# Down projections of two feed-forward layers: three groups of four chunks by seven products of quarters, between plain pairs

## The chip, the core and the metric

The program runs on one core of a Trainium2 chip. The time is the device time of one execution in microseconds, the median of several runs. A profiled execution gives the rows that are quoted. Engines: PE (TensorE matrix multiplication, with its weight loads as PEld), DVE (VectorE), ACT (ScalarE), POOL (GpSimd), and SP, whose queue issues nearly all transfers.

## What is computed

Three transformer blocks follow one another on 1024 tokens of width 1024 in 32-bit floats. Blocks 1 and 3 end in a feed-forward layer of 2816 inner channels:

```python
# first block: causal convolution over three tokens on the up projection
up = causal_depthwise_conv(h @ w_up[l], conv_w[l], conv_b[l])
a, bgate = jnp.split(up, [D_FF], axis=-1)
x = x + (jax.nn.silu(a) * bgate) @ w_down[l]
# third block
gate, up = jnp.split(h @ w_gate_up, 2, axis=-1)
ffn = (jax.nn.silu(gate) * up) @ w_down
h = layer_norm_3(ALPHA * h + ffn, ln2_g[l], ln2_b[l])
```

The change concerns the products with `w_down` (2816 x 1024) in both layers. The function `ffn` writes both.

## The kernel before

Activations lie transposed, channels on the 128 partitions and tokens along the row, in two halves of 512 tokens. A 32-bit product is made from three passes: every operand is split into a high part, which ACT rounds (`ghi`, `whi`, `shi`), and a low part, the operand less its high part (`glo`, `wlo`, `slo`), made on POOL or DVE; PE adds high x high, low x high and high x low in one PSUM bank. One matmul is 128 x 128 by 128 x 512.

**The up projection** goes by seven products (Strassen's scheme in Winograd's form) in `strassen`: each weight tile of 1024 columns is cut in quarters, `s_steps` adds and subtracts them on POOL in six steps and splits them, and seven products take the place of eight. Its gated results `g` go out to DRAM (`gd<-g`).

**The down projection** comes behind it. The 2816 inner channels are 22 chunks of 128. The first 18 are taken as nine pairs in `down`: for each of eight row tiles `j` and two halves, six matmuls add two chunks into a fresh PSUM bank (`dn`; six banks in rotation, tag `b`), and DVE adds the bank to the running sum `X` (64 kept tiles of 128 x 512, tag `h`, hold `X`, `gx` and their parts). The four last chunks go another way, which stays as it is. For each pair two weight tiles are loaded (`raw`), split on ACT and POOL, and two chunks by two halves of gated products are read back (`gx<-gd`), and split, two on POOL and two on DVE. The work left from the last step of `strassen` (`self.left`: four convolutions with their gates in the first layer, one gate in the third) is done at every third group of the first pair.

**Order.** Instructions stand in the order in which Python writes them, engine by engine; nothing is reordered. SP's queue holds each transfer until its buffer is free, and what stands behind it waits too. `tail` issues, during the last seven-product step of the up projection, the loads of the first weights, of the first gated products and of `X`.

Of the kernel before, what the change touches and what calls it, by code (L numbers as in the profile page):

```python
# [9 lines left out]
F32 = mybir.dt.float32  # L10
F32R = mybir.dt.float32r
AF = mybir.ActivationFunctionType
ALU = mybir.AluOpType
# [7 lines left out]
NFF = FF // 128  # L21
# [18 lines left out]
def _weights(a):  # L40
    def wa(name, lo, hi):
        return list(_chunks_a(a[name][0][:, lo:hi]))

    def wb(name, lo, hi):
        return list(_chunks_b(a[name][0][:, lo:hi]))

    def abba(tiles):
        return tiles + tiles[0:4]

    def ffn(up, down):  # L50
        ab = _chunks_a(a[up][0])
# [247 lines left out]
class Kernel:  # L299
# [14 lines left out]
    def bank(self, name="bank"):  # L314
        return self.ps.tile([128, 512], F32, tag="b", name=name)
# [957 lines left out]

    def s_dma(self, n):

        pool = self.up if (n + self.lead) % 2 else self.wp
# [82 lines left out]
    def ffn(self, evac, put, later, add_last, done, by_half, alpha=None, lead=2):  # L1359
# [3 lines left out]
        nc, X, G = self.nc, self.X, {}  # L1363
        from contextlib import ExitStack
        with ExitStack() as ctx:
# [33 lines left out]
            def g_group(i):  # L1399
                cs = (2 * i, 2 * i + 1) if i < NFF // 2 - 2 else range(NFF - 4, NFF)  # L1400
                return [(c, half, i % 2 and c < NFF - 1) for c in cs for half in range(2)]

            def x_load(j):
                for half in range(2):
                    X[j][half] = self.h("X")
                    nc.sync.dma_start(out=X[j][half], in_=self.x2d[j][:, HF * half:HF * half + HF])

            def tail(n):

                if n == 0:  # L1410
                    del self.stops[0]
                    self.wi += 2 * (NFF - lead)
                    self.w_load()
                    self.w_load()
                elif n == 1:
                    for a in g_group(0):
                        g_dma(*a[:2])
                    for j in range(2):
                        x_load(j)
                elif n == 2:  # L1420
                    for j in range(2, 5):
                        x_load(j)
                else:
                    for a in g_group(0):
                        g_split(*a, nc.gpsimd)
# [24 lines left out]
            def down(i, ws):  # L1450
                n = 0
                loads = g_group(i + 1)
                gap = 12 // len(loads)
                for j in range(8):
                    for half in range(2):
                        ps = self.bank("dn")
                        for k in range(2):
                            whi, wlo = ws[k]
                            ghi, glo = G[2 * i + k, half]
# [6 lines left out]
                        if alpha and i == 0:  # L1466
# [9 lines left out]
            for i in range(NFF // 2 - 2):  # L1476
                ws = self.w_take(2)
                if i == 0:
                    self.w_retire(0)
                yield from down(i, ws)  # L1480
                if i < NFF // 2 - 3:
                    for a in g_group(i + 2):
                        g_dma(*a[:2])
                self.w_retire(2)
# [1018 lines left out]
```

## Time and profile before

| | us |
|---|---|
| median of 3 runs | 3134.41 (3132.58 to 3134.44) |
| profiled execution, device time | 3128.57 |
| its span | 3126.8 |
| PE busy in the span | 2948.0 |
| POOL busy in the span | 1428.8 |

The down projection of the first layer begins at 904 us of the span, that of the third at 2850 us. A row of the timeline has start, duration, engine, line and operation, out<-in with sizes, and in brackets the engine's idle time before it and what ended it.

### The profile page before, as it was taken

The page shows a single profiled execution, that of the slowest core. Times are in us where ns is not written, and L with a number is a line of the kernel's source. Part 1 is how long each engine was busy: PE and PEld are TensorE (multiplying, and loading weights), DVE is VectorE, ACT ScalarE, POOL GpSimd, SP SyncE. Part 2 cuts the span into 40 slices and gives each one's busy share as a digit, 9 for nine tenths or more (in the row PEclk, how much of TensorE's full clock was granted, in tenths as well). Part 3 has the DMA queues.
Part 4 walks back from the last instruction along what each step waited for, and adds up shares of the span by engine and source line. Part 5 has one row for each costly group of instructions (what it writes and reads, how often), then busy time and mean ns, then how long its engine had stood idle before and what let it go on. Part 6 is the DMA issues. An engine that isn't in the chain of part 4 may idle for free. (4 is left out here: it accounts for less than half of the span.)

```text
span 3126.8 us, 41448 instructions
## 1 busy us (share of the span) xinstructions
PE 2948.0 (94%) x15222; PEld 2506.4 (80%) x15222; DVE 1797.5 (57%) x3512; ACT 1284.2 (41%) x2493; POOL 1428.8 (46%) x1006
## 2 busy tenths in 40 slices
PE   8999998999999999889998989998899899999997
PEld 7898776888878878868897778977688688888887
DVE  6444246666675569976645665577767522224556
ACT  4232224444431143556673356654444422222223
POOL 4313434777743365862214342144333477774330
PEclk9999999999999999999999999999889999999998
DMA  4101241222252312131113232110223222225321
GB/s 160 29 27 50 73 135 41 81 81 81 81 184 86 108 48 81 38 108 49 47 39 118 84 121 64 42 31 28 68 68 98 84 81 81 86 80 179 108 81 55
DMA packets 114876, 248.96 MB, mean 80 GB/s; under 512 B 19696, under 2 KB 31600, under 8 KB 114672
## 3 DMA queue, kind: packets, MB, share of 16 engines
q1 hardware_dynamic: 114384, 246.01, 24.0%
q8 instruction: 120, 1.97, 0.3%
q14 instruction: 84, 0.69, 0.1%
q10 hardware_dynamic: 288, 0.30, 0.0%
HBM read 192.52 MB, written 53.74 MB: 79 GB/s over the span
## 5 line engine op out<-in xcount | busy, mean ns | idle before, releaser
L332 POOL TENSOR_TENSOR wlo<-raw,whi 128x1024 fp32r<-128x1024 f32 x240 | 581.8, 2433 | 861.7 <-ACT whi L326 845.0
L326 ACT ACTIVATE whi<-raw 128x1024 fp32r<-128x1024 f32 x240 | 248.2, 1053 | 535.9 <-PE dn L347 283.7
L332 DVE TENSOR_TENSOR X<-dn,X 128x512 f32<-128x512 f32 (+1 forms) x312 | 209.8, 676 | 162.2 <-PE dn L347 159.9
L347 PE MATMUL dn<-ghi,whi 128*128 128x512 f32 (+1 forms) x736 | 281.7, 383 | 0.5 <-DVE X L332 0.5
L347 PE MATMUL dn<-glo,whi 128*128 128x512 f32 (+1 forms) x736 | 279.8, 380 | 0.0
L347 PE MATMUL dn<-ghi,wlo 128*128 128x512 f32 (+1 forms) x736 | 279.8, 380 | 0.0
L332 POOL TENSOR_TENSOR raw<-raw 128x512 f32<-128x512 f32 x156 | 203.0, 1301 | 12.1
L332 POOL TENSOR_TENSOR slo<-raw,shi 128x512 fp32r<-128x512 f32 x117 | 150.6, 1301 | 105.6 <-ACT shi L326 104.4
L347 PE MATMUL p<-thi,shi 128*128 128x512 f32 x468 | 184.7, 395 | 13.4 <-DVE u L1132 9.7
L332 DVE TENSOR_TENSOR v<-p,e 128x512 f32<-128x512 f32 x78 | 53.8, 689 | 243.6 <-ACT e L326 194.2
L347 PE MATMUL p<-hhi,wlo 128*128 128x512 f32 x468 | 182.2, 389 | 1.7 <-POOL wlo L332 1.7
L347 PE MATMUL p<-tlo,shi 128*128 128x512 f32 x468 | 183.2, 391 | 0.0
L347 PE MATMUL p<-thi,slo 128*128 128x512 f32 x468 | 183.1, 391 | 0.0
L347 PE MATMUL p<-hhi,whi 128*128 128x512 f32 x468 | 182.1, 389 | 0.0
L347 PE MATMUL p<-hlo,whi 128*128 128x512 f32 x468 | 182.1, 389 | 0.0
L329 DVE SCALAR_TENSOR_TENSOR t<-u,vec,t 128x512 f32<-128x512 f32 x176 | 132.9, 755 | 79.4 <-ACT t L326 74.1
L347 PE MATMUL qk<-hhi,whi 128*128 128x512 f32 x384 | 164.5, 429 | 7.7 <-ACT hhi L326 7.0
L332 POOL TENSOR_TENSOR beta<-beta,f 128x511 f32<-128x511 f32 (+3 forms) x96 | 90.3, 945 | 155.7 <-DVE beta L336 146.5
L347 PEld LDWEIGHTS dn<-ghi,whi 128*128 128x128 f32 x736 | 138.8, 189 | 27.9 <-DVE X L332 0.9
L347 PEld LDWEIGHTS dn<-glo,whi 128*128 128x128 f32 x736 | 138.7, 188 | 26.3
L347 PEld LDWEIGHTS dn<-ghi,wlo 128*128 128x128 f32 x736 | 138.6, 188 | 26.1
L347 PE MATMUL qk<-hlo,whi 128*128 128x512 f32 x384 | 154.9, 403 | 1.3 <-DVE hlo L329 1.3
(404 smaller groups left out, 8156.9 us busy)
## 6 DMA issues: line engine op xcount, KB each, us to landing
raw<-in_wall SPq DMA_DIRECT2D x240, 512.0 KB, 3.8
gd<-g SPq DMA_DIRECT2D x88, 256.0 KB, 2.1
gx<-gd SPq DMA_DIRECT2D x88, 256.0 KB, 5.1
x2d<-X SPq DMA_DIRECT2D x64, 256.0 KB, 2.0
X<-x2d SPq DMA_DIRECT2D x64, 256.0 KB, 5.3
x<-in_xT SPq DMA_DIRECT2D x16, 256.0 KB, 5.9
X<-in_xT SPq DMA_DIRECT2D x16, 256.0 KB, 4.1
T<-in_rpbx SPq DMA_DIRECT2D x8, 448.0 KB, 4.1
```

The lines of the kernel that those rows point to most:

```text
L326: self.nc.scalar.activation(out=out, in_=in_, func=func, bias=bias, scale=scale, **kw)
L329: self.nc.vector.scalar_tensor_tensor(out=out, in0=in0, scalar=s, in1=in1, op0=op0, op1=op1)
L332: (eng or self.nc.vector).tensor_tensor(out=out, in0=in0, in1=in1, op=op)
L347: self.nc.tensor.matmul(out=out, lhsT=lhsT, rhs=rhs, start=start, stop=stop, skip_group_check=more)
```

## The change

In place of nine pairs there are three rounds, each of one pair (function `two`, 16 groups of six matmuls as before) and one group of four chunks (two calls of `seven`, 14 groups of six matmuls each). The order of chunks is 2, 4, 2, 4, 2, 4, and the last four as before. I call the three parts of a round the pair, the first and the second half; each half serves half of the row tiles.

For a group of four, the weights are laid out on the host so that a tile holds 256 output channels of four chunks, and `s_steps` makes the sums of quarters on POOL, as in the up projection. The gated products' sums (`b_steps`: 5, 6, 7 and 4 are differences, 1, 2 and 3 plain) are made on DVE, one at a time between the evacuations; their high parts are ACT's, the low parts of the differences DVE's, those of the plain ones POOL's. In `seven`, bank `c` takes products 1, 6, 7 and 4 on top of one another; DVE adds what stands in it to `X` after each, and PE goes on in the same bank. Products 5 and 3 share `f`, product 2 has `d`, each with two banks, six in all. The work left from the up projection is done in the first groups of the first pair, one function at each. Loads change places: only two weight tiles are loaded ahead of the first gated products, then two tiles for the first half among `X`, and eight `gx` behind `X` in place of four.

```diff
@@ in _weights, ffn
-        out.extend(dn[:NFF - 4])
+        for i in range(0, NFF - 4, 6):
+            out.extend(dn[i:i + 2])
+            for col in (0, 512, 256, 768):
+                out.append(np.concatenate([dn[k][:, col:col + 256] for k in range(i + 2, i + 6)], axis=1))
-S_TILES = ((38, 38), (178, 180))
+S_TILES = ((38, 38), (78, 78), (178, 180), (220, 220))
@@ in Kernel.ffn
+            pairs = [(i, i + 1) for i in range(0, NFF - 4, 6)]
+            quads = [range(i + 2, i + 6) for i in range(0, NFF - 4, 6)]
...
                 elif n == 1:
-                    for a in g_group(0):
-                        g_dma(*a[:2])
+                    g_raw(pairs[0])
                     for j in range(2):
                         x_load(j)
+                    self.s_raws(self.up)
...
-                    for a in g_group(1):
-                        g_dma(*a[:2])
+                    g_raw(quads[0])
+                    self.s_raws(self.wp)
...
+                def raw(n, o, half):
+                    return [lambda k=k: self.tt(*pair(n, k, G[cs[o + k], half]), ALU.subtract, nc.gpsimd)
+                            for k in range(2)]
+
+                def made(n, out, parts):
+                    low = {}
+
+                    def diff(k):
+                        p, q = parts(k)
+                        x = out(k)
+                        self.tt(x, p, q, ALU.subtract)
+                        low[k] = pair(n, k, x)
+
+                    return [lambda: diff(0), lambda: diff(1), lambda: self.tt(*low[0], ALU.subtract),
+                            lambda: self.tt(*low[1], ALU.subtract)]
...
+                return (raw(1, 0, 0) + made(5, bank, lambda k: (G[cs[k], 1], G[cs[k], 0])),
+                        made(6, lambda k: t[k], lambda k: (G[cs[2 + k], 1], t[k])) + raw(2, 2, 0) +
+                        made(7, lambda k: G[cs[k], 1], lambda k: (G[cs[2 + k], 1], G[cs[k], 1])),
+                        raw(3, 2, 1) + made(4, lambda k: t[k], lambda k: (G[cs[2 + k], 0], t[k])))
...
@@ in two (was down)
-                        if n % 3 == 1 and self.left:
-                            self.left.pop(0)()
-                        if n % gap == 0 and loads and n > 2:
-                            g_split(*loads.pop(0))
+                        if self.left:
+                            self.left.pop(0)()
+                        for f in todo.get(n, ()):
+                            f()
...
+            def seven(s, A, B, todo):
+                banks, n = {}, 0
+                plan = ((1, "c", "A1", 0, 0, 0), (5, "f", "S1", 0, 4, 1), (6, "c", "S24", 0, 0, 1),
+                        (2, "d", "A1", 512, 0, 0), (7, "c", "S3", 0, 4, 1), (3, "f", "S24", 512, 0, 1),
+                        (4, "c", "A22", 0, 4, 0))
+                for p, key, w, off, row, half in plan:
+                    for m in range(2):
+                        start = (key, m) not in banks
+                        if start:
+                            banks[key, m] = self.bank("dn")
+                        ps = banks[key, m]
...
+                            self.mm(ps, whi[:, c], hi, start and k == 0, False, not start)
+                            self.mm(ps, whi[:, c], lo, False, False, not start)
+                            self.mm(ps, wlo[:, c], hi, False, k == 1, not start)
...
+                        self.tt(x, ps, x, ALU.add)
+                        for f in todo.get(n, ()):
+                            f()
+                        n += 1
...
+                        at((0, 2, 4, 6, 8, 10) if s is None else (0, 1, 2, 5, 7, 10), self.s_steps(u + 1, nxt))
+                if s is None:
+                    if u == 0:
+                        at((2, 3, 4, 5, 6, 7), b0)
+                    at((8, 9, 10, 11, 9, 11, 12, 13, 14, 15) if u == 0 else (0, 1, 3, 4, 5, 6, 7, 9, 11, 13), b1)
+                elif s == 0:
+                    at((0, 1, 1, 3, 5, 7), b2)
...
+                elif more:
+                    at((0, 1, 2, 3), [lambda c=c, h=h: g_split(c, h, False, nc.gpsimd)
+                                      for c in pairs[i + 1] for h in range(2)])
+                    nb = {}
+                    b0, b1, b2 = b_steps(quads[i + 1], nb)
+                    at((5, 6, 7, 9, 11, 13), b0)
```

The numbers in `at` are the groups of six matmuls after which a step is written.

The next rows show DVE at the start of the first layer's down projection. Of before, from the first evacuation on (`STT` work on `t` and `g` belongs to the convolutions):

```order
L332 TENSOR_TENSOR X<-dn,X 128x512
L1132 MEMSET u 128x2
L1134 COPY carry<-u 128x2
L329 SCALAR_TENSOR_TENSOR t<-u,vec,t 128x512 x2
L332 TENSOR_TENSOR X<-dn,X 128x512 x3
L1136 COPY u<-carry 128x2
L329 SCALAR_TENSOR_TENSOR t<-u,vec,t 128x512 x2
L332 TENSOR_TENSOR X<-dn,X 128x512 x2
L332 TENSOR_TENSOR glo<-gx,ghi 128x512
```

Of the change, from the second evacuation on:

```order
L335 TENSOR_TENSOR X<-dn,X 128x512
L1139 COPY u<-carry 128x2
L332 SCALAR_TENSOR_TENSOR t<-u,vec,t 128x512 x2
L335 TENSOR_TENSOR X<-dn,X 128x512
L1135 MEMSET u 128x2
L1137 COPY carry<-u 128x2
L332 SCALAR_TENSOR_TENSOR t<-u,vec,t 128x512 x2
L335 TENSOR_TENSOR g<-t,a 128x512
L335 TENSOR_TENSOR X<-dn,X 128x512
L1139 COPY u<-carry 128x2
L332 SCALAR_TENSOR_TENSOR t<-u,vec,t 128x512 x2
L335 TENSOR_TENSOR g<-t,a 128x512
```

The convolutions now stand behind each of the first four evacuations, where they stood behind the first, the fourth, the seventh and the tenth.

POOL, of before, from a pair's weights to the next pair's (`raw` are weight tiles, `gx` gated products):

```order
L332 TENSOR_TENSOR wlo_7499<-raw_7294,whi_7498 128x1024
L332 TENSOR_TENSOR wlo_7505<-raw_7300,whi_7504 128x1024
L332 TENSOR_TENSOR glo_7544<-gx_7454,ghi_7543 128x512
L332 TENSOR_TENSOR glo_7617<-gx_7458,ghi_7616 128x512
L332 TENSOR_TENSOR wlo_7697<-raw_7502,whi_7696 128x1024
L332 TENSOR_TENSOR wlo_7703<-raw_7508,whi_7702 128x1024
```

Of the change, in the second round's pair (the steps for the first half, and product 2's low parts among them):

```order
L335 TENSOR_TENSOR slo_8083<-raw_7920,shi_8082 128x512
L335 TENSOR_TENSOR raw_7920<-raw_7920 128x512
L335 TENSOR_TENSOR raw_7920<-raw_7918,raw_7920 128x512
L335 TENSOR_TENSOR slo_8130<-raw_7920,shi_8129 128x512
L335 TENSOR_TENSOR slo_8134<-raw_7920,shi_8133 128x512
L335 TENSOR_TENSOR glo_8147<-gx_7889,ghi_8146 128x512
L335 TENSOR_TENSOR wlo_8159<-raw_7918,whi_8158 128x1024
L335 TENSOR_TENSOR glo_8163<-gx_7893,ghi_8162 128x512
L335 TENSOR_TENSOR raw_7918<-raw_7920,raw_7918 128x512
L335 TENSOR_TENSOR raw_7918<-raw_7918 128x512
L335 TENSOR_TENSOR wlo_8209<-raw_7918,whi_8208 128x1024
```

Two low parts of 1024 columns and two of 512 were a pair's whole work; now a pair has eleven operations on POOL, four of them sums of quarters on `raw`.

DVE, of before, in the first layer's second pair:

```order
L332 TENSOR_TENSOR X_7334<-dn_7708,X_7334 128x512
L332 TENSOR_TENSOR X_7336<-dn_7716,X_7336 128x512
L332 TENSOR_TENSOR X_7338<-dn_7724,X_7338 128x512
L332 TENSOR_TENSOR X_7340<-dn_7736,X_7340 128x512
L332 TENSOR_TENSOR X_7390<-dn_7744,X_7390 128x512
L332 TENSOR_TENSOR X_7392<-dn_7752,X_7392 128x512
```

Of the change, in the first half of the first round (`dn_7748` and `dn_7764` are the two banks `c`):

```order
L335 TENSOR_TENSOR X_7330<-dn_7748,X_7330 128x512
L335 TENSOR_TENSOR X_7334<-dn_7764,X_7334 128x512
L335 TENSOR_TENSOR t_7606<-gx_7462,t_7606 128x512
L335 TENSOR_TENSOR X_7400<-dn_7782,X_7400 128x512
L335 TENSOR_TENSOR X_7444<-dn_7798,X_7444 128x512
L335 TENSOR_TENSOR t_7619<-gx_7466,t_7619 128x512
L335 TENSOR_TENSOR X_7332<-dn_7748,X_7332 128x512
L335 TENSOR_TENSOR X_7336<-dn_7764,X_7336 128x512
L335 TENSOR_TENSOR glo_7780<-t_7606,ghi_7779 128x512
L335 TENSOR_TENSOR X_7330<-dn_7837,X_7330 128x512
L335 TENSOR_TENSOR X_7334<-dn_7845,X_7334 128x512
```

Each evacuation read a bank of its own; now bank `dn_7748` is read, written on and read again, and the differences (`t`) and their low parts stand between.

## Rows read from the trace of the kernel before

**Rows 1.** Page, section 1: busy us, share of the span, instructions.

```profile
PE 2948.0 (94%) x15222; PEld 2506.4 (80%) x15222; DVE 1797.5 (57%) x3512; ACT 1284.2 (41%) x2493; POOL 1428.8 (46%) x1006
```

**Rows 2.** Busy time by stretch: up projection, then down projection of the first layer.

```profile
core 0: us, PE busy (x) PEld busy (x) DVE busy (x) ACT busy (x) POOL busy (x), PEclk, DMA share, GB/s
...
700.00:750.00 50.00, 50.00 (x222) 41.42 (x221) 33.37 (x57) 23.79 (x36) 37.49 (x26) 1.00 0.20 69
...
904.00:925.00 21.00, 20.48 (x90) 16.59 (x89) 16.29 (x29) 7.21 (x11) 8.60 (x6) 1.00 0.70 265
925.00:946.00 21.00, 21.00 (x93) 17.14 (x92) 15.03 (x24) 4.55 (x6) 7.82 (x4) 1.00 0.50 163
...
967.00:988.00 21.00, 21.00 (x94) 17.39 (x93) 11.57 (x18) 4.09 (x6) 7.27 (x4) 1.00 0.30 101
```

**Rows 3.** Waits of PE, 2840 to 3110 us, then 880 to 1160 us.

```profile
PE ln L347 <- DVE lsq L332: 2.6, 1, 2.6
...
PE dn L347 <- DVE X L332: 0.5, 1, 0.5
```

**Rows 4.** Timeline of PE, first and second pair of the first layer.

```profile
904.00 0.39 PE L347 MATMUL dn<-ghi,whi 128*128 128x512 f32 x1
...
922.38 0.50 PE L347 MATMUL dn<-ghi,whi 128*128 128x512 f32 x1 [0.52 <-DVE X L332]
...
926.72 0.47 PE L347 MATMUL dn<-ghi,whi 128*128 128x512 f32 x1
...
932.26 0.39 PE L347 MATMUL dn<-ghi,whi 128*128 128x512 f32 x1
```

**Rows 5.** Timeline of ACT, weights of two pairs of the third block.

```profile
2870.36 2.01 ACT L326 ACTIVATE whi<-raw 128x1024 fp32r<-128x1024 f32 x2 [7.32 <-PE dn L347]
...
2892.12 2.01 ACT L326 ACTIVATE whi<-raw 128x1024 fp32r<-128x1024 f32 x2 [17.67 <-PE dn L347]
```

**Rows 6.** Page, section 5: busy us, mean ns of one, idle time before.

```profile
L332 POOL TENSOR_TENSOR wlo<-raw,whi 128x1024 fp32r<-128x1024 f32 x240 | 581.8, 2433 | 861.7 <-ACT whi L326 845.0
L326 ACT ACTIVATE whi<-raw 128x1024 fp32r<-128x1024 f32 x240 | 248.2, 1053 | 535.9 <-PE dn L347 283.7
...
L332 POOL TENSOR_TENSOR raw<-raw 128x512 f32<-128x512 f32 x156 | 203.0, 1301 | 12.1
```

**Rows 7.** Timeline of DVE, first and second pair of the first layer.

```profile
909.00 1.88 DVE L332 TENSOR_TENSOR X<-dn,X 128x512 f32<-128x512 f32 x3
...
915.26 1.55 DVE L329 SCALAR_TENSOR_TENSOR t<-u,vec,t 128x512 f32<-128x512 f32 x2 [4.30 <-ACT t L326]
...
932.46 0.69 DVE L332 TENSOR_TENSOR X<-dn,X 128x512 f32<-128x512 f32 x1 [0.50 <-PE dn L347]
```

**Rows 8.** Timeline of ACT, the same place.

```profile
909.13 0.60 ACT L326 ACTIVATE a<-t 128x512 f32<-128x512 f32 x1 [3.38 <-DVE t L329]
913.92 0.63 ACT L326 ACTIVATE ghi<-gx 128x512 fp32r<-128x512 f32 x1 [4.19 <-DMA gx<-gd]
914.46 0.77 ACT L326 ACTIVATE t<-u,vec 128x512 f32<-128x512 f32 x1
```

**Rows 9.** Timeline of SP's queue before and in the first pair.

```profile
893.87 1.82 SPq L1390 DMA_DIRECT2D gx<-gd  x4
...
908.58 2.30 SPq L1390 DMA_DIRECT2D gx<-gd  x4
```

**Rows 10.** Timelines of POOL, then of DVE: low parts and squares side by side.

```profile
900.19 5.07 POOL L332 TENSOR_TENSOR glo<-gx,ghi 128x512 fp32r<-128x512 f32 x4 [6.77 <-ACT ghi L326]
...
1084.36 5.97 POOL L332 TENSOR_TENSOR glo<-gx,ghi 128x512 fp32r<-128x512 f32 x4
...
1088.11 1.07 DVE L332 TENSOR_TENSOR glo<-gx,ghi 128x512 fp32r<-128x512 f32 x1
...
1093.55 0.68 DVE L332 TENSOR_TENSOR glo<-gx,ghi 128x512 fp32r<-128x512 f32 x1
...
1118.77 1.77 DVE L332 TENSOR_TENSOR s<-s,s 128x512 f32<-128x512 f32 x1
```

More of the change, by code (lines that the diff above doesn't have):

```diff
@@ L1274, in s_dma, with s_raws @@
     def s_dma(self, n):
-        pool = self.up if (n + self.lead) % 2 else self.wp
+        self.s_raws(self.up if (n + self.lead) % 2 else self.wp)
+    def s_raws(self, pool):
         for _ in range(2):
@@ L1397, in g_split, with g_raw @@
                 G[c, half] = hi, lo
-            def g_group(i):
-                cs = (2 * i, 2 * i + 1) if i < NFF // 2 - 2 else range(NFF - 4, NFF)
-                return [(c, half, i % 2 and c < NFF - 1) for c in cs for half in range(2)]
+            def g_raw(cs):
+                for c in cs:
+                    for half in range(2):
+                        g_dma(c, half)
+            pairs = [(i, i + 1) for i in range(0, NFF - 4, 6)]
+            quads = [range(i + 2, i + 6) for i in range(0, NFF - 4, 6)]
+            ends = range(NFF - 4, NFF)
             def x_load(j):
@@ L1423, in tail @@
                 else:
-                    for a in g_group(0):
-                        g_split(*a, nc.gpsimd)
+                    for c in pairs[0]:
+                        for half in range(2):
+                            g_split(c, half, False, nc.gpsimd)
                     for j in range(5, 8):
                         x_load(j)
-                    for a in g_group(1):
-                        g_dma(*a[:2])
+                    g_raw(quads[0])
+                    self.s_raws(self.wp)
             yield from self.first_quad(lambda i, half, ps: evac(i // 2, i % 2, half, ps), hook)
@@ L1448, in ffn, with b_steps, pair, bank @@
             yield from self.strassen(put, left, later, (lambda: next(gt)) if lead == 2 else (lambda: None), tail)
-            def down(i, ws):
+            def b_steps(cs, B):
+                t = [None, None]
+                def pair(n, k, src):
+                    hi, lo = self.h("ghi", F32R), self.h("glo", F32R)
+                    B.setdefault(n, ([None] * 2, [None] * 2))
+                    B[n][0][k], B[n][1][k] = hi, lo
+                    self.act(hi, src, AF.Copy)
+                    return lo, src, hi
+                def raw(n, o, half):
[10 more added lines that the diff above has]
+                            lambda: self.tt(*low[1], ALU.subtract)]
+                def bank(k):
+                    t[k] = self.pt.tile([128, 512], F32, tag="t", name="t")
+                    return t[k]
+                return (raw(1, 0, 0) + made(5, bank, lambda k: (G[cs[k], 1], G[cs[k], 0])),
+                        made(6, lambda k: t[k], lambda k: (G[cs[2 + k], 1], t[k])) + raw(2, 2, 0) +
+                        made(7, lambda k: G[cs[k], 1], lambda k: (G[cs[2 + k], 1], G[cs[k], 1])),
+                        raw(3, 2, 1) + made(4, lambda k: t[k], lambda k: (G[cs[2 + k], 0], t[k])))
+            def p_steps(W):
+                def whole():
+                    raw = self.sraws.pop(0)
+                    hi = self.wp.tile([128, 1024], F32R, tag="whi", bufs=4, name="whi")
+                    lo = self.wp.tile([128, 1024], F32R, tag="wlo", bufs=4, name="wlo")
+                    self.split(hi, lo, raw)
+                    W.append((hi, lo))
+                return [whole, whole]
+            def two(cs, ws, todo):
                 n = 0
-                loads = g_group(i + 1)
-                gap = 12 // len(loads)
                 for j in range(8):
@@ L1458, in down @@
                             whi, wlo = ws[k]
-                            ghi, glo = G[2 * i + k, half]
+                            ghi, glo = G[cs[k], half]
                             c = slice(128 * j, 128 * j + 128)
@@ L1465, in down @@
                         x = X[j][half]
-                        if alpha and i == 0:
+                        if alpha and cs[0] == 0:
                             self.stt(x, x, alpha, ps, ALU.mult, ALU.add)
@@ new lines, in ffn, with at, turn @@
+            units = [u for i in range(len(quads)) for u in ((i, None), (i, 0), (i, 1))]
+            W, B = self.w_take(2), {}
+            b0, b1, b2 = b_steps(quads[0], B)
+            for u, (i, s) in enumerate(units):
+                todo, nxt = {}, []
+                def at(slots, fs):
+                    for x, f in zip(slots, fs):
+                        todo.setdefault(x, []).append(f)
+                if 0 < u and u + 2 < len(units):
+                    self.s_raws(self.up if u % 2 else self.wp)
+                if u + 1 < len(units):
+                    if units[u + 1][1] is None:
+                        at((2, 6), p_steps(nxt))
+                    else:
+                        nxt = {}
+                        at((0, 2, 4, 6, 8, 10) if s is None else (0, 1, 2, 5, 7, 10), self.s_steps(u + 1, nxt))
+                more = i + 1 < len(quads)
+                if s is None:
[4 more added lines that the diff above has]
+                    at((0, 1, 1, 3, 5, 7), b2)
+                    if more:
+                        at((4, 10), [lambda: g_raw(pairs[i + 1]), lambda: g_raw(quads[i + 1])])
+                    else:
+                        at((4, 8, 9, 10, 11), [lambda: g_raw(ends)] + [lambda c=c: g_split(c, 0, False) for c in ends])
+                elif more:
[4 more added lines that the diff above has]
+                    at((5, 6, 7, 9, 11, 13), b0)
+                else:
+                    def turn():
+                        del self.stops[0]
+                        self.wi += 2 * (len(units) - 1)
+                        self.w_load()
+                        self.w_load()
+                    at((0, 3, 5, 7, 9), [turn] + [lambda c=c: g_split(c, 1, c < NFF - 1) for c in ends])
+                if s is None:
+                    yield from two(pairs[i], W, todo)
+                    if u == 0:
+                        self.w_retire(2)
+                else:
+                    yield from seven(s, W, B, todo)
+                    if s and more:
+                        B = nb
+                W = nxt
@@ L1485, in ffn @@
+            self.w_retire(0)
             full, q0, q1 = slice(0, HF), slice(0, HF // 2), slice(HF // 2, HF)
```

15 lines of the change are left out of this document (6 added, 9 removed).

## The prediction, made before the change was run

> **What bounds the kernel now.** I read the page first: PE is busy for 94% of the span, no other engine for more than 57% [rows 1]. The table by stretch then tells whether that holds where the change is made: in the down projection PE is busy for 21.00 us of 21, DVE for about 12, POOL for 7 and ACT for 4, and the granted clock is 1.00, the upper level of 2.4 GHz [rows 2]. The list of PE's waits is nearly empty there: 0.5 us in the first layer; in the third block's window the longest entry already belongs to the closing normalization [rows 3]. So both stages last as long as their matmuls are many. What is taken from PE is gained in full as long as POOL, DVE and ACT deliver in time.
>
> The price of a matmul comes from the beat of a pair: weights of two successive pairs are split at 2870.36 and 2892.12, each time when PE releases the buffer [rows 5]. That is 21.76 us for 16 groups of six, 1.36 us a group and 0.2267 us a matmul. A row's own 0.39 us [rows 4] overlaps its neighbours and is no price.
>
> **What the change removes.** Nine pairs are 9 x 96 = 864 matmuls. Three pairs and six halves of 84 are 288 + 504 = 792. That is 72 fewer in each layer, 144 in all, and 144 x 0.2267 = **32.6 us**. Shapes stay. The weight and gated bytes also stay: four weight tiles and eight gated tiles for four chunks, before and after, so I give the transfers as a whole no price.
>
> **What it adds beside PE.** I take a round (a pair and two halves: 21.76 + 2 x 19.04 = 59.8 us of PE).
>
> POOL makes for each half three low parts of 512 columns and four sums of quarters at 1.30 us, and two low parts of 1024 at 2.43 [rows 6]: 7 x 1.30 + 2 x 2.43 = 14.0 us. A round is 2 x 14.0, a pair's weights 4.9, six low parts of plain products 7.8 and four of the pair's 5.2, together **45.8 us of 59.8**. The three pairs that it replaces held some 22 us of 65 [rows 2]. That it fits beside a full PE shows in the up projection, which has the same six steps for every 84 matmuls: POOL 37.5 of 50 us, PE 50 of 50 [rows 2].
>
> DVE has 44 evacuations and 16 differences and low parts a round, 60 operations at a pitch of 0.60 us (three in 1.88 us, [rows 7]): 36 of 59.8 us. ACT: seven high parts of 1024 or their equal, 2 x (3 x 0.63 + 2 x 1.05) + 2 x 1.05 + 18 x 0.63 = 21 us [rows 6, 8]. Neither is short on average; the first pair is, in the first layer.
>
> **The first pair of the first layer.** Now PE loses 1.0 us there: its seventeenth group starts at 926.72, against 904.00 + 16 x 1.36 = 925.76 [rows 4], after one wait at 922.38 for an evacuation. The cause is the four convolutions left over, each a chain over ACT and DVE: DVE idles 4.30 us at 915.26 for ACT's `t`, and ACT has stood 4.19 us at 913.92 for `gx` [rows 7, 8]. The change puts the four chains behind the first four evacuations. I walk it. The first ends at 909.0, as now. For the second, ACT does the gate's 0.60 at 909.13, one high part, then `t` (0.77): 911.2; DVE two operations (1.55) and the second evacuation: 913.4. The third has the same chain, and one product more: third and fourth evacuation around 914 and 916.9, where they now end by 910.9. Group 10 must have the fourth's bank (six banks): it wants to start at 904 + 9 x 1.36 = 916.2, and is 0.7 late. Behind it `gx` and the last convolution give the fifth evacuation at 919.8; group 11 wants it at 917.6: **2.2 late**. From there DVE has an evacuation and one difference or low part a group, 1.20 against 1.36 us, and keeps its lag to the end of the pair. In the first half product 6 comes back to bank `c` three groups after product 1 left it, 4.1 us; two evacuations and the last low parts of the pair are ahead, another 0.9 late. In all 3.1 us against 1.0 now: a **loss of 2.1 us**. Bounds: better than now by 1.0 if DVE slips through; worse by 8.6 if all of the pair's DVE work (28 operations at 0.6, four chains of about 3.4 us with ACT's turns: 30.4 us) lies on a path of 21.76. I take the walk, since the next half needs only 14 + 4 operations, 10.8 of 19.0 us, and takes the rest up. The third block has one gate left over: 0.
>
> **Loads.** Eight `gx` follow `X` where four did. In the old order their issue began at 908.58 and ACT had the first at 913.92 [rows 8, 9]. The first four `gx` (893.87 now, behind four weight tiles of which two waited for POOL) go earlier, since only two tiles stand ahead, and take 1.8 us out of the queue; two weight tiles go in. So the first arrives at about the same time, the eighth some 5 us later. On POOL in the first pair I count from 914.5: plain low part, another, two of 512, one of 1024, two sums, one plain, the last of 1024, with the waits for ACT it ends near 932. Product 6 wants it at 928 + 5.4 = 933.4. Cover: 1.5 us, the thinnest of the kernel; later halves have 2 to 7 us. Cost 0; a load 4 us late would cost 2.5.
>
> **DVE and POOL side by side.** Four low parts on POOL take 5.07 us at 900.19, but 5.97 at 1084.36, where DVE makes two of its own; one of these takes 1.07 instead of 0.68, and a sum of two squares 1.77 [rows 10]. Operations of DVE with both inputs in SBUF do this; the evacuations read one input from PSUM. The change has six such a round (differences 5 and 7, low parts of 7), 36 in all, with POOL busy three quarters of the time. POOL then has 45.8 + 6 x 0.45 = 48.5 us, which still fits. For DVE lower bound 0, since DVE's wait of up to 1.1 us is mostly covered by six banks. Upper: in the second half two differences stand three to four groups ahead of the last evacuation, and 2 x 1.1 - 0.5 = 1.7 us could reach PE, at six places 10 us. I take **1.0 us**: at 1088 DVE's delay moved no group of PE [rows 3].
>
> The Trainium skill, SBUF — State Buffer, section Who interferes with whom, goes further: a DVE instruction with two SBUF inputs and a GpSimd instruction that reads SBUF exclude each other for a whole instruction. The stretched rows agree in kind; its result is the third case below.
>
> **Sum.** 32.6 - 2.1 - 1.0 = 29.5 us. The profiled execution took 3128.57, so 3099.1; it lies 5.8 below the median of the runs (3134.41), and with the same distance the median becomes **3105 us**, 0.94% less.
>
> **The cases.**
> 1. As forecast, 3099 to 3111: 0.70. Lower end: 32.6 + 1.0 gained is 3100.8, with a microsecond of scatter 3099.
> 2. POOL comes late again and again. For: 77% of a round, little cover in the first pair. Against: each half has 2 us or more to catch up, as the up projection shows. If `gx` is 4 us late and every one of 12 halves then loses 1 us: 2.5 + 12 = 14.5 us, 3119. Chance 0.12.
> 3. DVE stands for whole POOL operations. Two differences in each second half each wait for a low part of 1024 (2.43): 4.9 us less the 1.9 that the banks cover is 3 us, at six places 18: 3123. The rows show 0.4 to 1.1 rather than 2.4 [rows 10]. This is the skill's rule taken at its worst. Chance 0.09.
> 4. Slower. Each half opens on the bank that the group before last has just filled: one group, 1.36 us, for an evacuation that begins 0.2 us after the group (932.46, where the next group began at 932.26) and takes 0.69 [rows 4, 7]. Cover 0.47. If DVE stands just then at a low part whose high part ACT holds back behind a weight tile that waits for POOL's two sums (2 x 1.30 + 1.05), PE loses 3.7 us at each of 12 seams and more: 44 us, so 3105 + 44 = 3149. From 2.5 us a seam (29.5 / 12) nothing is left. Against it: in the last two groups of a first half nothing but evacuations is written, in a second half one low part behind the last. Chance of slower 0.05, of no change 0.03.
>
> That the matmuls do not become fewer is no case: the order of PE's instructions has 144 rows less.
>
> Faster or slower means by over 0.2%, about 6 us, which is what a measurement here tells from none. Cases 1 to 3 are faster: 0.92 with a hundredth for what I haven't thought of. The range goes from 3099 to 3119 and leaves out part of case 3, case 4 and little else.
>
> **What would show it.** Right: 144 fewer `dn` matmuls; PE at 21.00 of 21 us in every stretch from the second round on; POOL near 16 of 21; waits of PE on DVE of some 3 us at 917 to 935 and nearly none in the third block. Wrong: PE waiting for POOL's `wlo`, or for `X` at the start of every half (cases 2 and 4), DVE differences of 2 us and more (case 3), a `gx` that comes after 918.

## The result, and the profile after

The changed kernel takes 3106.85 us (median of 4 runs, 3100.14 to 3112.1), against 3134.43 us for the kernel before in the same comparison (4 runs, 3132.58 to 3138.46): a ratio of 0.9915, interval 0.9903 to 0.9927. It is faster by 0.85%. The profiled execution took 3106.03 us with a span of 3104.2. Section 1 of its page answers to [rows 1]:

```profile
PE 2917.8 (94%) x15078; PEld 2480.3 (80%) x15078; DVE 1828.4 (59%) x3552; ACT 1326.4 (43%) x2565; POOL 1569.8 (51%) x1110
```

PE has 144 instructions less, POOL 104 more, and POOL is busy 141 us longer. The busy time by stretch of the first layer answers to [rows 2]. The first two stretches are the first round's pair and its seam; the stretch that follows and one of the second round (967) stand for the rest:

```profile
core 0: us, PE busy (x) PEld busy (x) DVE busy (x) ACT busy (x) POOL busy (x), PEclk, DMA share, GB/s
904.00:925.00 21.00, 19.83 (x88) 16.10 (x87) 18.62 (x34) 8.51 (x14) 12.75 (x11) 1.00 0.77 275
925.00:946.00 21.00, 17.51 (x67) 13.93 (x66) 18.31 (x26) 9.39 (x15) 20.64 (x14) 0.84 0.59 201
946.00:967.00 21.00, 21.00 (x94) 17.41 (x93) 12.02 (x18) 6.71 (x10) 18.11 (x12) 1.00 0.29 100
967.00:988.00 21.00, 21.00 (x94) 17.38 (x94) 16.51 (x25) 6.17 (x11) 13.14 (x10) 1.00 0.01 1
...
934.00:938.00 4.00, 0.51 (x3) 0.24 (x2) 4.00 (x6) 1.90 (x4) 3.88 (x3) 0.82 0.95 272
938.00:943.00 5.00, 5.00 (x12) 3.90 (x13) 3.33 (x6) 3.27 (x5) 4.92 (x5) 0.50 0.93 344
943.00:948.00 5.00, 5.00 (x23) 4.08 (x21) 3.75 (x6) 0.00 (x0) 4.92 (x4) 0.96 0.47 177
```

PE is at 21.00 of 21 again from 946 on; the nine stretches of 21 us of the third block's down projection, 2838 to 3027, all show 21.00. The loss lies in 904 to 946, where PE is short of 4.7 us, and in 938 to 943 the granted clock is 0.50: the lower level, 1.2 GHz, with 12 matmuls in 5 us where the next five, at 0.96, have 23. The row of 934 to 938 already has 0.82, though PE went on only at 937.79: the clock fell while PE was still waiting. The list of PE's waits from 905 to 1136 us, the whole stage, has one line (total, times, longest), which answers to [rows 3]:

```profile
PE dn L350 <- DVE X L335: 4.7, 2, 3.5
```

The timeline of PE has the stage's start, both waits and what follows the second; it answers to [rows 4]:

```profile
905.47 0.39 PE L350 MATMUL dn<-ghi,whi 128*128 128x512 f32 x1
...
918.85 0.39 PE L350 MATMUL dn<-ghi,wlo 128*128 128x512 f32 x1
920.41 0.50 PE L350 MATMUL dn<-ghi,whi 128*128 128x512 f32 x1 [1.17 <-DVE X L335]
...
933.91 0.39 PE L350 MATMUL dn<-ghi,slo 128*128 128x512 f32 x1
937.79 0.77 PE L350 MATMUL dn<-ghi,whi 128*128 128x512 f32 x1 [3.49 <-DVE X L335]
938.36 0.63 PE L350 MATMUL dn<-glo,whi 128*128 128x512 f32 x1
938.78 0.63 PE L350 MATMUL dn<-ghi,wlo 128*128 128x512 f32 x1
...
943.44 0.39 PE L350 MATMUL dn<-glo,whi 128*128 128x512 f32 x1
```

By the beat of 0.2267 us the group at 920.41, the eleventh, should have begun at 919.08, so it is 1.33 us late. Product 6, at 937.79, should have begun at 934.14 and is 3.65 late. From there 13 matmuls, to 943.44, take 5.65 us instead of 2.95: another 2.70. What DVE did before the second wait, and POOL at the same time (its rows are in the experiments' part on product 7), answers to [rows 10]:

```profile
919.67 0.68 DVE L335 TENSOR_TENSOR X<-dn,X 128x512 f32<-128x512 f32 x1
...
929.85 1.02 DVE L335 TENSOR_TENSOR gx<-gx 128x512 f32<-128x512 f32 x1
930.79 0.68 DVE L335 TENSOR_TENSOR X<-dn,X 128x512 f32<-128x512 f32 x1
931.39 2.28 DVE L335 TENSOR_TENSOR gx<-gx 128x512 f32<-128x512 f32 x1
933.60 0.68 DVE L335 TENSOR_TENSOR X<-dn,X 128x512 f32<-128x512 f32 x1
934.20 1.17 DVE L335 TENSOR_TENSOR glo<-gx,ghi 128x512 fp32r<-128x512 f32 x1
935.29 0.68 DVE L335 TENSOR_TENSOR X<-dn,X 128x512 f32<-128x512 f32 x1
935.89 1.15 DVE L335 TENSOR_TENSOR glo<-gx,ghi 128x512 fp32r<-128x512 f32 x1
936.97 1.27 DVE L335 TENSOR_TENSOR X<-dn,X 128x512 f32<-128x512 f32 x2
```

The four operations of product 7 (two differences `gx<-gx`, two low parts) take 5.62 us, where one takes 0.68 elsewhere. PE's product 6 waits for the evacuation behind the last of them.

How much each stage changed can be read more finely than from the runs, because the stages with changed code repeat from run to run while the rest doesn't. The next table gives, from PE's timeline in microseconds, the first layer's stage (first to last `dn` matmul), the third block's (first `dn` to the first matmul on `acc` of the closing normalization), and the unchanged code between them:

| kernel | first layer | third block | between |
|---|---|---|---|
| before | 240.19 | 220.47 | 1705.07 |
| changed | 230.66 | 204.16 | 1708.29 |
| changed, two more profiles | 230.61, 230.57 | 204.16, 204.15 | 1703.07, 1711.94 |

72 matmuls less in each stage are 16.3 us. The third block has all of it (16.31). The first layer has 9.53, so it lost 6.8 us more than before.

### The profile page after: what moved, and what is told of

Same layout as the page of the kernel before. It is cut to its first block, busy times and chain, and to the rows that moved or that the text cites. A ratio compares the mean times of both kernels' runs of the same rounds, so it can differ in the third digit from the quotient of the medians.

```text
span 3104.2 us, 41331 instructions
## 1 busy us (share of the span) xinstructions
PE 2917.8 (94%) x15078; PEld 2480.3 (80%) x15078; DVE 1828.4 (59%) x3552; ACT 1326.4 (43%) x2565; POOL 1569.8 (51%) x1110
## 5 line engine op out<-in xcount | busy, mean ns | idle before, releaser
L335 POOL TENSOR_TENSOR raw<-raw 128x512 f32<-128x512 f32 x204 | 268.3, 1315 | 15.0
L335 POOL TENSOR_TENSOR slo<-raw,shi 128x512 fp32r<-128x512 f32 x153 | 200.4, 1324 | 147.8 <-ACT shi L329 146.5
L335 DVE TENSOR_TENSOR X<-dn,X 128x512 f32<-128x512 f32 (+1 forms) x288 | 193.5, 674 | 115.5 <-PE dn L350 111.2
L350 PE MATMUL dn<-ghi,whi 128*128 128x512 f32 (+1 forms) x544 | 208.8, 384 | 4.7 <-DVE X L335 4.7
L350 PE MATMUL dn<-glo,whi 128*128 128x512 f32 (+1 forms) x544 | 206.6, 380 | 0.0
L350 PE MATMUL dn<-ghi,wlo 128*128 128x512 f32 (+1 forms) x544 | 206.5, 380 | 0.0
L350 PE MATMUL op<-hhi,wlo 128*128 128x512 f32 x384 | 153.2, 399 | 4.0 <-POOL wlo L335 4.0
L350 PE MATMUL op<-hhi,whi 128*128 128x512 f32 x384 | 155.6, 405 | 0.0
L350 PE MATMUL qk<-hhi,wlo 128*128 128x512 f32 x384 | 154.8, 403 | 0.0
```

Of the source, the lines that this page charges most:

```text
L335: (eng or self.nc.vector).tensor_tensor(out=out, in0=in0, in1=in1, op=op)
L350: self.nc.tensor.matmul(out=out, lhsT=lhsT, rhs=rhs, start=start, stop=stop, skip_group_check=more)
```

## The experiments

The theory after the result: the first layer's loss comes from the work that DVE has in the first pair (convolutions and product 7's operations that stand for POOL), the lower clock is a consequence of the wait, and nothing else is lost. Rivals: the loss is in the loads or in POOL; the late rounds also lose, hidden in the scatter; a seam has little cover.

**The changed kernel once more**, for the scatter:

> The changed kernel once more, to see how far its runs scatter: they went from 3100.1 to 3112.1 us. If the scatter comes from the place of the change, its own profile shows other waits of PE in the first round of the first layer than 1.17 and 3.49 us, or another stretch at the lower clock; if it comes from elsewhere, these stay within 0.3 us and the rest of the span differs. I expect the latter, and a median of 3104 to 3109 us.

Measured: 3107.85 us (6 runs, 3099.83 to 3116.06) against 3131.6; ratio 0.9929, interval 0.9917 to 0.9941. The profile of its fastest run, 3099.83 us, has the same two waits (1.21 and 3.43 us) and the same stages as the profile of 3106.03 (table above). The scatter is thus not made by the down projections: in the three profiles of this kernel their stages agree within 0.1 us, while the unchanged code between them takes 1703 to 1712 us. The slowest runs, up to 3116 us, have no profile.

**Less DVE work in the first pair.** Two of the three operations of each of the four left-over convolutions are left out, eight on DVE (so the last of the 22 chunks misses two taps):

```diff
-            self.stt(t, u[:, 1:HF + 1], self.v("conv_w1", ch), t, ALU.mult, ALU.add)
-            self.stt(t, u[:, 0:HF], self.v("conv_w0", ch), t, ALU.mult, ALU.add)
+            if c < NFF - 1:
+                self.stt(t, u[:, 1:HF + 1], self.v("conv_w1", ch), t, ALU.mult, ALU.add)
+                self.stt(t, u[:, 0:HF], self.v("conv_w0", ch), t, ALU.mult, ALU.add)
```

> Leaves out two of three taps of the convolution for the last of the 22 chunks, eight DVE operations of some 0.75 us at the start of the first layer's down projection. Theory A (all of DVE's work in the first pair counts, the four convolutions and the operations for product 7 that wait for POOL): the wait of 1.17 us before group 11 goes, the wait of 3.49 us before product 6 shrinks to 0.5 to 1.5, and the 13 matmuls at half the clock go with it: 5 to 6.5 us less than the changed kernel. Theory B (the convolutions alone): both waits go entirely, 7 us less. Theory C (bank c taken up again after three groups is too early whatever DVE did before): the second wait stays above 3 us, 1.5 us less.

Measured: 3104.46 us, ratio 0.9913 (0.9901 to 0.9926); the first layer's stage 224.40 us, 6.2 less. Its timelines of PE and DVE:

```profile
931.83 0.47 PE L350 MATMUL dn<-ghi,whi 128*128 128x512 f32 x1 [1.31 <-DVE X L335]
```

```profile
925.38 2.29 DVE L335 TENSOR_TENSOR gx<-gx 128x512 f32<-128x512 f32 x1
```

The wait ahead of group 11 is gone, that at product 6 is down to 1.31 and the lower clock doesn't come, as theory A had it. The medians show less, 3.4 us against the changed kernel's 3107.85 in the same comparison, which is within the scatter of the runs. The 2.29 us of the difference is the same as before the edit. So the lateness is the sum of two things, the convolutions and the stretched operations of product 7: without the first, the second alone is nearly covered. Loads and POOL were not changed and cost nothing here.

**What the stretched operations wait for.** POOL's rows of the changed kernel beside DVE's above:

```profile
929.00 1.32 POOL L335 TENSOR_TENSOR glo<-gx,ghi 128x512 fp32r<-128x512 f32 x1
930.25 2.88 POOL L335 TENSOR_TENSOR wlo<-raw,whi 128x1024 fp32r<-128x1024 f32 x1
933.09 1.73 POOL L335 TENSOR_TENSOR glo<-gx,ghi 128x512 fp32r<-128x512 f32 x1
934.94 1.56 POOL L335 TENSOR_TENSOR slo<-raw,shi 128x512 fp32r<-128x512 f32 x1
```

POOL's four rows end at 930.32, 933.13, 934.82 and 936.50. DVE's four operations with both inputs in SBUF end at 930.87, 933.67, 935.37 and 937.04: each 0.54 or 0.55 us behind the end of the POOL row that was running when it began. An evacuation, with one input from PSUM, stands between each two and takes its 0.68 beside a running POOL row. POOL is longer too, 2.88 instead of 2.44 on the average of the page, and 1.73 and 1.56 instead of 1.3. So such an operation of DVE waits until POOL's whole instruction is over: the longest took 1.60 us more than 0.68, where POOL's row had 1.74 us still to run. The Trainium skill (SBUF — State Buffer, section Who interferes with whom) states that a DVE instruction with two SBUF inputs contends with a GpSimd instruction that reads SBUF, and that the port pair which they share is an exclusive lock. The trace agrees, with these ends.

**Product 7's sums later**, in the first half behind groups 1, 3, 5 and 7, in the first round:

```diff
-                    at((8, 9, 10, 11, 9, 11, 12, 13, 14, 15) if u == 0 else (0, 1, 3, 4, 5, 6, 7, 9, 11, 13), b1)
+                    at((8, 9, 10, 11, 9, 11) if u == 0 else (0, 1, 3, 4, 5, 6, 7, 9, 11, 13), b1)
+                    if u == 1:
+                        at((0, 2, 4, 6), b1[6:])
```

> In the first round of both layers the two differences and two low parts of product 7 are written in the first half (behind its groups 1, 3, 5 and 7) and no longer at the end of the pair; nothing is left out. Theory A: the wait before group 11 stays at 1.2 us, the wait before product 6 shrinks from 3.5 to under 0.7, since four operations with 5.6 us of DVE time are no longer ahead of it, and the clock stays at its upper level: 5 to 6 us less than the changed kernel in the first layer, nothing in the third block. Theory B: the second wait stays near 3 us and the time the same. Theory C: the same as B.

Measured: 3106.32 us, ratio 0.9919 (0.9907 to 0.9931); first layer 228.93 us, third block 208.17, 4.0 more than the changed kernel. Theory A was right for the two old waits (1.21 us ahead of group 11, none at product 6), but two others have come, at product 7. Timelines of PE and of ACT:

```profile
941.05 0.49 PE L350 MATMUL dn<-ghi,shi 128*128 128x512 f32 x1 [1.09 <-ACT ghi L329]
942.88 0.50 PE L350 MATMUL dn<-glo,shi 128*128 128x512 f32 x1 [1.34 <-DVE glo L335]
```

```profile
938.14 0.63 ACT L329 ACTIVATE shi<-raw 128x512 fp32r<-128x512 f32 x1 [3.57 <-POOL raw L335]
939.84 0.63 ACT L329 ACTIVATE shi<-raw 128x512 fp32r<-128x512 f32 x1 [1.07 <-POOL raw L335]
940.38 0.61 ACT L329 ACTIVATE ghi<-gx 128x512 fp32r<-128x512 f32 x1
```

Product 7's high part stood on ACT behind two `shi` that wait 4.6 us for POOL's sums of weights. Product 7's sums can thus stand too early for DVE, in the pair, or too late for ACT, in the half, and the room between is narrow. The third block's 4.0 us are a wait of 2.12 us at 2881.54 for a low part on DVE and the lower clock behind it.

**Product 7's sums in between**, behind groups 1 to 4 of the first half:

```diff
-                        at((0, 2, 4, 6), b1[6:])
+                        at((0, 1, 2, 3), b1[6:])
```

> As the run that moved the sums of product 7 into the first half, but behind its groups 1, 2, 3 and 4, so that ACT's high parts stand ahead of those that wait for POOL's sums of quarters; nothing is left out. If the waits of that run at product 7 came from ACT's order, they go: the first layer's stage (first to last dn matmul) shrinks from 230.7 to 225 +- 1 us, with the wait of 1.2 us before group 11 left, and the third block's stays at 204.2. If moving these operations only moves the wait, product 7 or product 6 still waits 2 us or more and the stage stays above 228.

Measured: 3102.36 us (3091.84 to 3105.16), ratio 0.9902 (0.9885 to 0.9919); first layer 224.33 us, third block 204.16. The only wait left in either stage is that of group 11, and there is no lower clock:

```profile
919.66 0.50 PE L350 MATMUL dn<-ghi,whi 128*128 128x512 f32 x1 [1.18 <-DVE X L335]
```

So product 6's wait and the lower clock behind it cost 6.3 us in the changed kernel, and the wait of group 11 alone brings no lower clock.

To see it in whole times, this kernel and the changed one ran again on one chip, in five rounds:

> The changed kernel beside the next one on the same chip, to tell a few us apart: stage of the first layer 230.6 us, of the third block 204.2 us, median 3103 to 3109 us.

> The version with product 7's sums in the first half, unchanged, beside the changed kernel: stage of the first layer 224.3 us, of the third block 204.2. If the 6.3 us of the stage reach the end, the median is 5 to 8 us below the changed kernel's; if the code between the two layers gives them back, the medians differ by less than 3 us.

Measured: 3108.81 us (ratio 0.9939, 0.9926 to 0.9953) for the changed kernel, 3101.13 us (ratio 0.991, 0.9897 to 0.9924) with product 7's sums in between. The difference of the medians is 7.7 us, that of the stages 6.24 (230.57 and 224.33). This version beats both kernels.

**The convolutions spread as well**, behind groups 1, 3, 5 and 7 of the pair, the sums for products 5 and 6 moved behind them:

```diff
-                        if self.left:
+                        if n % 2 == 0 and self.left:
...
-                        at((2, 3, 4, 5, 6, 7), b0)
-                    at((8, 9, 10, 11, 9, 11) if u == 0 else (0, 1, 3, 4, 5, 6, 7, 9, 11, 13), b1)
+                        at((2, 3, 7, 8, 9, 10), b0)
+                    at((11, 12, 13, 14, 9, 11) if u == 0 else (0, 1, 3, 4, 5, 6, 7, 9, 11, 13), b1)
```

> As the run before, and in the first pair the four convolutions stand behind groups 1, 3, 5 and 7 and the sums of products 5 and 6 after them (groups 8 to 15); nothing is left out. If the wait before group 11 comes from four chains over ACT and DVE in a row, it goes, and the first layer's stage comes to 223.0 to 224.5 us, that is within 1 us of what its 1004 matmuls need. If DVE's sum of work in that pair is too much in any order, a wait of 1 to 3 us comes later, at product 5 or 6. Kernel some 7 us faster than the changed one, 3100 +- 3.

Measured: 3105.57 us, ratio 0.9922 (0.9908 to 0.9936); stage 225.84. The stage missed the 223.0 to 224.5 us forecast and the median the 3100 +- 3 (the stage has 984 matmuls, 223.1 us, not the 1004 of the expectation). The wait of group 11 is gone and two others stand further on, at products 6 and 7, as the rival had it in kind:

```profile
930.90 0.47 PE L350 MATMUL dn<-ghi,whi 128*128 128x512 f32 x1 [0.77 <-DVE X L335]
...
937.69 0.47 PE L350 MATMUL dn<-ghi,shi 128*128 128x512 f32 x1 [1.02 <-DVE X L335]
```

The wait moves, it doesn't go: by the table of stretches DVE is busy for 38.4 us of the 42 from 904 to 946 here, so little is left in which an order could hide the rest. That no order could is not shown.

**The third block alone changed**; the first layer has its nine pairs back (the former function, kept as `ffn_old`, and its layout of weights):

```diff
-        yield from self.ffn(evac, put, later, add_last, done2, last, lead=3)
+        yield from self.ffn_old(evac, put, later, add_last, done2, last, lead=3)
```

> The change in the third block alone; the first layer has its nine pairs back. If the third block gets all of its 72 matmuls (16.3 us) and the first layer lost 6.7 of its 16.3: 3134.4 - 16.3 = 3118 us, 11 us over the changed kernel. If both layers had lost alike, it would be 3134.4 - 13.8 = 3120.6.

Measured: 3118.32 us (3109.82 to 3119.96), ratio 0.995 (0.9938 to 0.9962); stages 239.98 and 204.15. The medians differ by 13.3 us and the third block's stage by 16.3, as long as the whole change makes it; the first layer's is as before. Against the changed kernel's 3107.85 us in the same comparison it is 10.5 us slower, forecast 11. So the two layers can be read apart, and the first layer's share of the change is its own stage's 9.5 us.

**POOL made fuller.** Two more additions of 1024 columns in every half, ahead of the last split of the weights:

```diff
         def s5():
+            if self.down:
+                for _ in range(2):
+                    self.tt(rb, rb, rb, ALU.add, P)
             st["S24"] = whole(ra)
```

> Every half gets two more POOL additions of 1024 columns (2.4 us each) on a tile that nothing reads any more, ahead of the last split of its weights; the result is unchanged. POOL then has some 48 + 29 = 77 us of work counted for the six halves' makers less what the pair leaves, that is about 58 us a round against 59.8 of PE. My theory (average work decides, slack passes from part to part): in the third block PE waits little, under 5 us over the whole down projection. Rival (each half must have its sums within its own span, case 2): the first half's weights come some 2 to 5 us late in every round and PE waits for wlo at product 6 each time, 10 to 25 us in the third block.

Measured: 3116.58 us (4 runs), ratio 0.9948 (0.9928 to 0.9967); stages 234.56 and 212.90. Some stretches of 19 us of the third block:

```profile
2872.00:2891.00 19.00, 18.64 (x83) 15.12 (x82) 15.73 (x22) 5.50 (x9) 18.84 (x12) 1.00 0.66 222
2891.00:2910.00 19.00, 18.16 (x80) 14.74 (x79) 10.53 (x16) 8.02 (x12) 18.84 (x12) 1.00 0.29 84
...
2992.00:3011.00 19.00, 19.00 (x86) 15.73 (x85) 13.06 (x19) 5.96 (x10) 18.77 (x14) 1.00 0.00 0
3011.00:3030.00 19.00, 14.57 (x61) 11.72 (x60) 8.99 (x10) 5.64 (x8) 16.54 (x9) 0.90 0.36 109
```

POOL is full, 18.8 of 19 us, and yet PE idles only 1.2 us in the first two stretches and not at all in the one that ends at 3011. Then some 7 of the 8.7 us go at once. Its last wait, and what ACT and DVE waited for:

```profile
3028.19 0.79 PE L350 MATMUL dn<-ghi,shi 128*128 128x512 f32 x1 [4.43 <-DVE X L335]
```

```profile
3019.43 1.06 ACT L329 ACTIVATE whi<-raw 128x1024 fp32r<-128x1024 f32 x1 [7.95 <-DMA raw<-in_wall]
```

```profile
3025.16 2.37 DVE L335 TENSOR_TENSOR glo<-gx,ghi 128x512 fp32r<-128x512 f32 x1 [6.11 <-ACT ghi L329]
```

POOL gives the weight tiles free late (SP's queue waits 14.5 us for its additions on them, 6.5 in the changed kernel), the loads for the last four chunks come late, ACT holds the next high parts behind them, and the evacuations stand behind DVE's low part. The loss in the third block is larger than my theory's 5 us and below the rival's 10 to 25, and it comes through a transfer, at one place, not a little in each half.

The first layer of this run also shows what the stretched operations alone do. DVE's work is the same as in the changed kernel, but POOL runs its two additions beside product 7's operations. These take 1.00, 1.78, 1.78 and 2.22 us, 6.78 together instead of 5.62, each ending 0.54 or 0.55 us behind a POOL row as before; and PE's wait at product 6 grows with them, from 3.49 to 4.62 us, 1.13 more for 1.16 more. The last of the four, and PE:

```profile
936.62 2.22 DVE L335 TENSOR_TENSOR glo<-gx,ghi 128x512 fp32r<-128x512 f32 x1
```

```profile
939.59 0.77 PE L350 MATMUL dn<-ghi,whi 128*128 128x512 f32 x1 [4.62 <-DVE X L335]
```

**DVE held up at the seam.** Four more additions behind group 12's evacuation in every half:

```diff
                         self.tt(x, ps, x, ALU.add)
+                        if n == 11:
+                            for _ in range(4):
+                                self.tt(self.R[1], ps, x, ALU.add)
```

> Behind the evacuation of group 12 of every half four more DVE additions stand (bank and running sum into a tile that nothing reads); the result is unchanged. Theory of the seam (case 4): the evacuation of group 13 then begins some 2.4 us late, its bank is the first of the next half, cover 0.47 us: PE waits 1.0 to 2.0 us at each of the six halves of a layer, 6 to 12 us in the third block, more where the clock falls. Rival (DVE has 7 us to spare in each half and takes it up): no wait at the seams and the stage within 1 us of 204.2.

Measured: 3104.69 us, ratio 0.9915 (0.9898 to 0.9932); stages 230.74 and 204.15: no loss. DVE and PE in the third block:

```profile
2886.04 0.69 DVE L335 TENSOR_TENSOR X<-dn,X 128x512 f32<-128x512 f32 x1 [0.67 <-PE dn L350]
2886.77 2.87 DVE L335 TENSOR_TENSOR R<-dn,X 128x512 f32<-128x512 f32 x4
2889.55 2.62 DVE L335 TENSOR_TENSOR X<-dn,X 128x512 f32<-128x512 f32 x4
```

```profile
2888.33 0.39 PE L350 MATMUL dn<-ghi,slo 128*128 128x512 f32 x1
2888.56 0.39 PE L350 MATMUL dn<-ghi,whi 128*128 128x512 f32 x1
```

PE opens the next half at 2888.56 without a wait, while the evacuation of group 13 begins only at 2889.55. The bank that it opens can't be the one that group 13 filled. Which one it is, the rows don't tell; one of those that the half left earlier is free by then.

## Why the prediction was right, and where its sum was not

The median came out at 3106.85, forecast 3105, within the range. By the steps:

- **144 matmuls less at 0.2267: right.** The third block's stage is shorter by 16.31 us, 72 x 0.2267 = 16.32, with nothing lost.
- **POOL, ACT and DVE fit on average: right.** POOL has 16.65 of 21 us on the mean of the third block's nine stretches, where "near 16" was forecast. The experiment with a fuller POOL shows where the room ends: with two additions more in every half (3.88 us the two, by its rows) POOL is full and the last loads come late.
- **The walk of the first pair, as far as group 11: right in kind, near in size, partly by luck.** Counted from PE's first matmul, the fifth evacuation was to end at 15.8 us (919.8 less 904.0) and ended at 14.9 (919.67 + 0.68, less 905.47); so group 11, put at 2.2 late, was 1.33 late. On the way the second evacuation was to end at 9.4 us and ended at 4.6: it did not stand behind ACT's chain, and errors cancelled.
- **"Another 0.9 late" at product 6: the term that was mis-sized.** It was 3.65. The walk gave product 7's operations the pace of the others (1.20 us for an evacuation and one operation). In fact all four stood for POOL, 2.9 us more than four times 0.68. From the fifth evacuation to the one that product 6 needs DVE took 17.30 us (919.67 to 936.97), where twelve at 1.20 are 14.4: the 2.9 is all of the difference, and without it 0.75 of the 3.65 is left. The prediction had priced the side-by-side work in another part, with waits of at most 1.1 us and only in second halves, and did not put it on the one path where nothing covered it. That both are needed is shown by the two experiments that take one away each: without the convolutions' work, or with product 7 elsewhere, the wait is 1.31 or none. That the stretch itself counts, and not only the four operations, is shown by the fuller POOL: 1.16 us more of it, 1.13 more of wait.
- **The lower clock was not in the sum at all:** 2.70 us behind that wait. The first pair's loss is then 1.33 + 3.65 + 2.70 = 7.7 us against 1.0 before, 6.7 more; the stages say 6.8, the prediction said 2.1.
- **"1.0 us" for DVE beside POOL elsewhere: it was 0.** There is no wait in later rounds nor in the third block. In the third block's first pair the same four operations took 5.61 us, one of them 2.29, but without the convolutions ahead of them the evacuation that product 6 needs ended 0.8 us before PE wanted the bank (2870.84 and 2871.62).
- **Loads: right, 0.** ACT's `ghi` at 914.11 has no wait for `gx` any more, where it stood 4.19 us in [rows 8].
- **Case 2** was not seen. When it was forced, it took another way than described: through the buffers and loads of the last chunks.
- **Case 3** was right in kind: DVE does stand for the rest of a whole POOL operation. A difference of 2.28 us, which the prediction names as a sign of being wrong, was seen. The case was priced at the wrong place: in the second halves the longest difference took 1.09 us and cost nothing, and in the first pair the stretch was most of the wait at product 6.
- **Case 4:** its premise, that a half opens on the bank filled by the group before last, fell with the experiment at the seam. Its cover is more than the 0.47 us given: DVE 2.87 us late cost nothing.

By the stages the gain is 25.8 us (9.53 + 16.31) instead of 29.5. That the median nevertheless hit within 2 us is partly luck: the three comparisons of this kernel give 27.6, 23.8 and 21.5 us between the medians, and 25.8 lies among them. Why the code between the layers takes 1703 to 1720 us in one profile or another was not tried, and stays open. Over all twelve profiles a longer stretch goes with more time at the lower clock: its mean granted clock is 0.956 in the shortest and 0.948 in the longest. Which of the two makes the other was not tried.

## What to carry to other kernels

When work is moved off a full PE, walk the first round behind the change's seam operation by operation: the average of later rounds tells nothing about the place where left-over work, first loads and new sums meet. Give each DVE operation with two SBUF inputs the rest of the POOL instruction that will be running, above all if that is a long one, and put those operations where PE still has evacuated banks ahead of it. A wait of PE of the length seen here, 2.1 us and more, should be priced with the matmuls that may follow it at the lower clock.

## What was not expected of the hardware

In each of the six waits of PE of 3.4 to 4.6 us in the down projections the granted clock fell to 0.50 before PE went on, and some 10 to 13 matmuls followed at 0.427 instead of 0.227 us. Single waits of 1.31 us and less, in all nine kernels, brought no such stretch. Between these the length of the wait does not decide alone: in the kernel with product 7's sums later a wait of 2.12 us in the third block was followed by a granted clock of 0.57, and so were two of 1.09 and 1.34 us close together in the first layer (943 below); in the kernel with the fuller POOL a wait of 2.98 us that ended at 1089.06 was followed by 1.00. A row of each of the two kernels:

```profile
943.00:947.00 4.00, 4.00 (x11) 3.17 (x12) 2.25 (x4) 0.00 (x0) 3.92 (x3) 0.57 0.39 148
```

```profile
1089.00:1093.00 4.00, 3.94 (x17) 3.28 (x18) 4.00 (x7) 1.00 (x1) 2.41 (x1) 1.00 0.32 123
```

What decides there was not tried.

The second thing is how exact the exclusion of DVE and POOL is: the ends of DVE's operations lie 0.54 to 0.55 us behind those of POOL's rows in all four instances of the first pair, and again in the third block (2864.53 + 2.29 against POOL's 2863.41 + 2.86). In five other traces every difference and low part of the down projections that took over 0.8 us ends 0.54 to 0.56 us behind.

```profile
2863.41 2.86 POOL L335 TENSOR_TENSOR wlo<-raw,whi 128x1024 fp32r<-128x1024 f32 x1
```

```profile
2864.53 2.29 DVE L335 TENSOR_TENSOR gx<-gx 128x512 f32<-128x512 f32 x1
```
